# A gated linear attention layer: the first gates' Silu put behind the first tile of the second queries, and other shares of the heads' steps for queries and keys

## The chip, the cores and the metric

The kernel runs on one core of a Trainium2 chip. The core has engines that work side by side, each through a queue of its own in order: TensorE (PE; the profile lists the loading of its weights apart, as PEld), VectorE (DVE), ScalarE (ACT), GpSimd (POOL) and SyncE (SP), which here only issues transfers. The metric is the device time of one execution in microseconds (us), in which all times below are given.

## What is computed

The reference is a decoder trunk of two layers on 512 tokens of width 1024, in float32: a latent attention layer, a gated linear attention layer (GLA), each followed by a squared-ReLU MLP, and a last norm. The change lies in the GLA layer:

```
h = xn @ w_in                      # q 512, k 512, v 1024, g 1024, a 16 columns
gk = log_sigmoid(a @ w_gk_up + b_gk) / 16
# 4 heads of 128 (keys) x 256 (values); b = cumulated gk; state S carried over the tokens
o = (q * exp(b)) @ S + causal(sum_d q k exp(b_t - b_s)) @ v
o = rms_norm(o, g_norm) * silu(g)
x = x + o @ w_o
```

## The kernel before, in words

Each product of two float32 matrices is made of three matmuls of high and low parts (`mm3`, L129 to L134): ACT writes the high part (L124), DVE the low one (L127).

In `gla` the input is projected in six pieces, in the order "vgqkVG" (`proj`, L1773). "v" is the first half of the values; "g" the first half of the gates, as seven products of 256 columns (`seven`, L1336, matmuls of L1344) in place of eight; "q" and "k" are the second half of the queries and keys (`proj_qk(1)` and `proj_qk(3)`, two tiles of 24 matmuls of 512 columns each, L132 to L134, and a DVE copy out, L1463 or L1466); "V" the second half of the values, again by `seven`; "G" the second half of the gates. The first half of the queries and keys is projected ahead of all this.

"g" leaves its sums raw: `g_done` copies them to eight tiles of 128x256 (L1428). `silu` (L1434) later turns all eight, in place, by an activation each (L1436). Silu lies in another table of ACT than Exp and Ln; a table load stands ahead of the first of them, and `exp_set` (L138) loads the old table behind the last. Each of these instructions goes through `keep_in_program_order`, which pins it behind the instruction that was written just before it on its engine. Exp and Ln are held behind the latest `exp_set` (`act_e`, L141). For the other instructions the written order is a rank, not an order: an instruction that is ready may be placed ahead of one that is written earlier.

The heads' work (`heads`, L1791) is a second generator. It is cut into steps, and after each unit that `proj` yields the pace is raised by `PACE` (L38) of its piece and one step is taken for each whole unit of pace. Heads 0 and 1 come first, interleaved:

- steps 1 to 12: six stages of the attention inside 128 tokens, for head 0 and head 1 in turn: pairs, fours (2), fours (8), halves (32), halves (64), turned. A stage makes its operands, and its products are written with the step after it. In the halves ACT copies an operand (tile E, L1643; one buffer), PE multiplies it (L1651), and ACT copies the blocks into A (L1657). "Turned" transposes the keys (L149, L1677) and splits them into tiles kth and ktl.
- step 13: the last products. Steps 14 to 17: `states` 0 (nine matmuls with the turned keys, L132 to L134, and sums of L1716 and L1720 whose parts go to tile S), `own_tiles` 0 (L1727, into two banks of tag "b"), `states` 1, `own_tiles` 1 (a bank of tag "b" and one of tag "c").
- step 18: `silu`, then `past` 0 (nine matmuls of L1727 with S). Step 19: `gated` 0, where ACT squares the outputs from their banks (L1748) and DVE multiplies them by the gates (L1750). Step 20: `gates` 2 (the decays of head 2, one matmul of L1544 and then Abs, Exp and Ln) and `past` 1. Step 21: `gated` 1. Step 22: `gates` 3 and the norm of head 0. Step 23: that of head 1. Then heads 2 and 3 follow in the same way.

Tag "b" has three banks of PSUM. `own_tiles` of heads 0 and 1 take all three, and the "V" piece takes three for its sums (z, w, y; L1362). In `seven` the first product goes to z, and ACT copies z to y behind it (L1347).

With `PACE` at 3.75 for "q" and "k" the steps fall so: 1 to 6 in "v" and "g", 7 to 9 after the first query tile, 10 to 13 after the second, 14 to 17 after the first key tile, 18 to 21 after the second, 22 to 26 in "V", the rest in "G".

Of the kernel before, what the change touches and what calls it, by code (L numbers as in the profile page):

```python
# [34 lines left out]
HV = 256  # L35
RANK = 16
EPS = 1e-6
PACE = {"v": 0.4, "g": 0.6, "q": 3.75, "k": 3.75, "V": 0.75, "G": 2.1}  # L38

Q_PART = 0.75  # L40
SCALE = (Q_PART / (NOPE + ROPE)) ** 0.5
# [9 lines left out]
def trunk_kernel(ctx: ExitStack, tc: tile.TileContext, t_in: dict, out: bass.AP):  # L51
# [86 lines left out]
    def exp_set():  # L138
        table[0] = tc.keep_in_program_order(ACT.preload_act_table_set("natural_log_exp_and_others"))
# [1103 lines left out]
    def gla(layer, nrm, vtag, ytag):  # L1243
# [49 lines left out]
        def b_type(c0, hf, done):  # L1293
            banks = [bank("b"), bank("b"), bank("b"), bank("ac"[hf])]

            def mms(w, kk, k, t):
                xk = cut(X[k], slice(None), slice(t * P, (t + 1) * P))
                mm3(banks[t], xk, cut(w, slice(None), kk), k == 0, k == ND - 1)

            for kc in range(2):  # L1300
                raw = load(
                    w_in[kc * 512 : (kc + 1) * 512, c0 + hf * 512 : c0 + hf * 512 + 512].rearrange("(k p) n -> p k n", p=P), 4, 512
                )
                for g in range(2):
                    w = piece(raw[:, 2 * g : 2 * g + 2], 2, 512, at=AT_SEVEN)
                    k0 = kc * 4 + g * 2
                    if k0 + 2 < ND:
                        for kk in range(2):
                            for t in range(NT):
                                mms(w, kk, k0 + kk, t)  # L1310
                            yield
                    else:
                        for t in range(NT):
                            for kk in range(2):
                                mms(w, kk, k0 + kk, t)
                            done(t, banks[t])
                            if t % 2:
                                yield
# [84 lines left out]
        G = {}  # L1403

        def g_done(hf):
            def room():
                t = gp.tile([P, 2 * NT * HV], F32, tag="g", bufs=1, name=f"g{hf}")
                G[hf] = [t[:, i * HV : (i + 1) * HV] for i in range(2 * NT)]
                return t

            def done_tile(t, p):
                if t == 0:
                    G["room"] = room()
                with tc.high_priority():
                    tc.keep_in_program_order(
                        ACT.activation(G["room"][:, t * S : (t + 1) * S], p, AF.Silu, scale=rtok[:, t : t + 1])
                    )
                    if t == NT - 1:
                        exp_set()
                if t == NT - 1:  # L1420
                    gdone.add(hf)

            def done(c, th, p):
                if hf not in G:
                    room()
                for i in range(2):
                    src, dst = p[:, i * HV : (i + 1) * HV], G[hf][2 * (2 * th + i) + c]
                    ACT.activation(dst, src, AF.Copy, scale=-1.0 if c else 1.0)  # L1428
                if (c, th) == (1, 0):
                    gdone.add(hf)  # L1430

            return done_tile if hf else done

        def silu():  # L1434
            for n, s in enumerate(G[0]):
                tc.keep_in_program_order(ACT.activation(s, s, AF.Silu, scale=rtok[:, n // 2 : n // 2 + 1]))  # L1436
            exp_set()

        def residual_back():
            x = residual_room("xT_back")  # L1440
            xT[:] = [x[:, j] for j in range(ND)]
            xall_of[0] = x
            for j in range(ND):
                POOL.dma_start(x[:, j], kept[:, j])
# [65 lines left out]
        V = {}  # L1510

        def v_done(hf):
            def done_tile(t, p):
                hi, lo = slot(vtag), slot(vtag)
                r = rtok[:, t : t + 1]
                ACT.activation(hi, p, AF.Copy, scale=r)
                DVE.scalar_tensor_tensor(lo, p, r, f(hi), ALU.mult, ALU.subtract)
                for c in range(2):
                    V[2 * hf + c, t] = cut((hi, lo), slice(None), slice(c * HV, (c + 1) * HV))
                if t == NT - 1:  # L1520
                    vdone.add(hf)

            if hf == 0:
                return done_tile

            def done(c, th, p):
                hi, lo = slot(vtag), slot(vtag)
                r_all = rtok_n if c else rtok
                for i in range(2):
                    cs = slice(i * HV, (i + 1) * HV)  # L1530
                    r = r_all[:, 2 * th + i : 2 * th + i + 1]
                    ACT.activation(hi[:, cs], p[:, cs], AF.Copy, scale=r)
                    DVE.scalar_tensor_tensor(lo[:, cs], p[:, cs], r, f(hi[:, cs]), ALU.mult, ALU.subtract)
                    V[2 * hf + c, 2 * th + i] = cut((hi, lo), slice(None), cs)
                if (c, th) == (1, 0):
                    vdone.add(hf)

            return done
# [234 lines left out]
        def proj():  # L1773
            parts = {
                "v": lambda: b_type(2 * DK, 0, v_done(0)),
                "g": lambda: seven(2 * DK + D, 0, g_done(0), both, ahead=2 * DK + FB),
                "q": lambda: proj_qk(1),
                "k": lambda: proj_qk(3),
                "V": lambda: seven(2 * DK + FB, 1, v_done(1), both),
                "G": lambda: b_type(2 * DK + D, 1, g_done(1)),  # L1780
            }
            for c in "vgqkVG":
                for _ in parts[c]():
                    if c == "v":
                        next(forming, None)
                    yield PACE[c]
                if c == "V":
                    residual_back()


        def heads():  # L1791
            for h in (0, 2):
                while any(i not in qk for i in (h, h + 1, 4 + h, 5 + h)):
                    yield
                late = None
                for two in zip(levels(h), levels(h + 1)):
                    for stage in two:
                        products = stage()
                        if late:
                            late()  # L1800
                        late = products
                        yield
                        if h and turning and 1 in vdone:
                            gather(turning.pop(0))
                            yield
                late()
                yield
                while h // 2 not in vdone:
                    yield

                def run(*stages):
                    for stage, r in stages:
                        stage(r)
                        yield

                if h == 0:
                    while 0 not in gdone:
                        yield
                    yield from run((states, 0), (own_tiles, 0), (states, 1), (own_tiles, 1))
                    silu()  # L1820
                    yield from run((past, 0), (gated, 0))
                    gates(2)
                    yield from run((past, 1), (gated, 1))
                    gates(3)
                else:
                    yield from run((states, 2), (own_tiles, 2), (past, 2), (states, 3))
                    while 1 not in gdone:
                        yield
                    yield from run((gated, 2), (own_tiles, 3), (past, 3), (gated, 3))
                yield from run((head_norm, h), (head_norm, h + 1))  # L1830
                if h:
                    begun.append(out_start(w_o, Y, 3, "bca"))
                    yield from run((gather, h))
                    begun[0][2](4)
                    yield from run((gather, h + 1))

        begun, turning = [], [0, 1]
        forming = quadrants()
        both = [sb.tile([P, S], F32, tag="acc", bufs=2, name=uname("weight_sum")).rearrange("p (k n) -> p k n", n=TH) for _ in range(2)]
        fetch(2 * DK + D, both, *SUM_2)  # L1840
# [3 lines left out]
        for _ in rest:  # L1844
            pass
        gates(1)
        main, side = proj(), heads()
        pace = 0.0
        for units in main:
# [43 lines left out]
    O, begun = mla(0, nrm, w0, mla_pools)  # L1893
# [23 lines left out]
    psum_layout(False)  # L1917
    slot_layout(SLOT_AT, 8)
    Y, begun = gla(0, n_mix1, "V", "B")
    n_mlp1 = Norm(ND, inv_dr, "mlp", ND)  # L1920
    out_proj(t_in["gla_w_o"][0], Y, n_mlp1, begun)
# [59 lines left out]
```

## Time and profile before

| | us |
|---|---|
| median of 3 runs | 1043.01 (1042.83 to 1043.1) |
| the profiled execution | 1042.12 |
| its span, first to last instruction | 1040.4 |
| PE busy | 1026.6 |
| DVE busy | 898.5 |
| ACT busy | 713.0 |
| PE busy between 571 and 690, the GLA layer from the second queries on | 114.5 of 119 |

"Busy" is the time in which an engine has an instruction at work, as a sum over the span. Idle time of an engine that nobody waits for costs nothing; what counts is where PE stands still, and for whom. In the lines below, "out<-in" names the tiles that are written and read without their buffer numbers, L is the line of the kernel, "xN" a number of like instructions that the line takes together, and a bracket at the end gives the idle time before it and what ended it. Times in such lines are from the span's start.

### The profile page before, as it was taken

The numbers are of one execution on the slowest core, as the hardware profiler recorded it, in microseconds if no ns is written. First come the engines' busy times: TensorE is split into PE (matmuls) and PEld (weight loads), VectorE is DVE, ScalarE is ACT, GpSimd is POOL, SyncE is SP. The second block draws the span as 40 slices with busy tenths as digits, with TensorE's granted clock in tenths as the row PEclk, the third lists the DMA queues.
The fourth block names the chain that finished last, engine by engine and source line by source line (L and its number), as shares of the span: only waits on it lengthen the run. The fifth ranks groups of instructions, "written<-read, shape, count | busy, mean of one in ns | idle before, by whom it ended". The sixth has DMA issues, their size and how long they took to land.

```text
span 1040.4 us, 17339 instructions
## 1 busy us (share of the span) xinstructions
PE 1026.6 (99%) x6666; PEld 925.6 (89%) x6666; DVE 898.5 (86%) x1387; ACT 713.0 (69%) x1178; POOL 120.3 (12%) x160
## 2 busy tenths in 40 slices
PE   9999999999999999999999989999999999999997
PEld 7788888899999999998889888888989989989986
DVE  7889976999989989989698679579799999898994
ACT  8667754676776776785475594765677677677784
POOL 7400000400101001002112110000000000000000
PEclk9999999999999999999999999999999999999999
DMA  7401214778677777626648643344568777777422
GB/s 234 123 21 41 79 45 152 196 198 214 175 203 201 182 201 197 150 82 184 170 89 186 141 122 133 106 97 148 143 201 198 191 195 199 195 190 187 119 82 81
DMA packets 74082, 157.40 MB, mean 151 GB/s; under 512 B 10160, under 2 KB 43952, under 8 KB 71440
## 3 DMA queue, kind: packets, MB, share of 16 engines
q1 hardware_dynamic: 57184, 115.66, 34.6%
q0 software_dynamic: 14720, 38.80, 20.9%
q10 hardware_dynamic: 2096, 1.84, 0.6%
q8 instruction: 52, 0.85, 0.3%
q14 instruction: 30, 0.25, 0.1%
HBM read 151.83 MB, written 4.19 MB: 150 GB/s over the span
## 4 chain that ended last, share of the span: by engine, by line
PE 83%; DVE 7%; ACT 4%; DMA 4%; issue 1%; SPq 0%; ACTq 0%; DVEq 0%; POOLq 0%
PE ps L992 25%; PE ps L1012 13%; PE ps L1005 13%; PE ps L132 7%; PE ps L133 7%; PE ps L134 7%; PE ps L1180 2%; DMA wraw<-in_gla_w_in_dram 2%; DVE wl L127 2%; PE ps L149 1%; PE ps L1344 1%; PE ps L1214 1%; ACT wh L124 1%; PE ps L1601 1%; PE ps L1727 1%
## 5 line engine op out<-in xcount | busy, mean ns | idle before, releaser
L124 ACT ACTIVATE wh<-wraw 128x1024 fp32r<-128x1024 f32 x141 | 148.2, 1056 | 99.5 <-issue 38.6
L127 DVE TENSOR_TENSOR wl<-wraw,wh 128x1024 fp32r<-128x1024 f32 x141 | 172.0, 1221 | 25.2 <-ACT wh L124 24.2
L992 PE MATMUL ps<-T,wh 128*128 128x256 f32 x896 | 154.8, 275 | 0.3
L127 DVE TENSOR_TENSOR wl<-comb,wh 128x1024 fp32r<-128x1024 f32 x112 | 136.6, 1221 | 14.4 <-ACT wh L124 14.4
L124 ACT ACTIVATE wh<-comb 128x1024 fp32r<-128x1024 f32 x112 | 118.6, 1059 | 43.3 <-issue 30.0
L992 PEld LDWEIGHTS ps<-T,wh 128*128 128x128 f32 x896 | 135.0, 188 | 0.8 <-ACT ps L1022 0.3
L992 PE MATMUL ps<-T,wl 128*128 128x256 f32 x448 | 123.3, 275 | 0.0
L1012 PE MATMUL ps<-wh,set 128*128 128x512 f32 x392 | 122.1, 390 | 0.0
L992 PE MATMUL ps<-set,wh 128*128 128x256 f32 x672 | 116.9, 276 | 0.0
L132 PE MATMUL ps<-set,wh 128*128 128x512 f32 x280 | 110.0, 393 | 0.0
L133 PE MATMUL ps<-set,wh 128*128 128x512 f32 x280 | 109.7, 392 | 0.0
L134 PE MATMUL ps<-set,wl 128*128 128x512 f32 x280 | 109.6, 392 | 0.0
L1005 PE MATMUL ps<-hidden_parts,wh 128*128 128x256 f32 x784 | 105.8, 275 | 0.0
L992 PEld LDWEIGHTS ps<-set,wh 128*128 128x128 f32 x672 | 102.0, 188 | 0.5
L1005 PEld LDWEIGHTS ps<-hidden_parts,wh 128*128 128x128 f32 x784 | 96.6, 188 | 0.0
L992 PE MATMUL ps<-set,wl 128*128 128x256 f32 x336 | 92.5, 275 | 0.0
L1012 PEld LDWEIGHTS ps<-wh,set 128*128 128x128 f32 x392 | 73.6, 188 | 15.3
L992 PEld LDWEIGHTS ps<-T,wl 128*128 128x128 f32 x448 | 84.1, 188 | 0.0
L1012 PE MATMUL ps<-wl,set 128*128 128x512 f32 x196 | 76.3, 389 | 0.0
L992 PEld LDWEIGHTS ps<-set,wl 128*128 128x128 f32 x336 | 63.1, 188 | 0.0
L133 PEld LDWEIGHTS ps<-set,wh 128*128 128x128 f32 x280 | 52.6, 188 | 11.2 <-DVE set L1770 0.4
L134 PEld LDWEIGHTS ps<-set,wl 128*128 128x128 f32 x280 | 52.6, 188 | 11.1 <-DVE wl L127 0.2
(456 smaller groups left out, 2276.9 us busy)
## 6 DMA issues: line engine op xcount, KB each, us to landing
comb<-in_mlp_w_down_dram SPq DMA_DIRECT2D x74, 512.0 KB, 4.4
wraw<-in_mlp_w_up_dram SPq DMA_DIRECT2D x18, 1024.0 KB, 4.9
wraw<-in_mlp_w_up_dram SPq DMA_DIRECT2D x28, 512.0 KB, 5.6
comb<-in_mlp_w_down_dram POOLq DMA_DIRECT2D x28, 512.0 KB, 7.2
wraw<-in_gla_w_in_dram SPq DMA_DIRECT2D x8, 1024.0 KB, 5.3
comb<-in_mlp_w_up_dram SPq DMA_DIRECT2D x14, 512.0 KB, 4.6
comb<-in_mlp_w_up_dram POOLq DMA_DIRECT2D x14, 512.0 KB, 6.8
wraw<-in_mlp_w_up_dram POOLq DMA_DIRECT2D x14, 512.0 KB, 7.5
```

The source lines that it names most:

```text
L124: order(ACT.activation(hi, src, AF.Copy))
L127: lo_eng.tensor_tensor(lo, src, f(hi), ALU.subtract)
L132: PE.matmul(psum, wh, xh, start=start, stop=False)
L133: PE.matmul(psum, wh, xl, start=False, stop=False)
L134: PE.matmul(psum, wl, xh, start=False, stop=stop)
L149: PE.transpose(psum, src, ident[: src.shape[0], : src.shape[0]])
L992: PE.matmul(o, a_, x_, start=start and j == 0 and k == 0 and n == 0, stop=k == KH - 1 and n == 2, skip_group_check=True)
L1005: PE.matmul(o, w_[:, k, j * P : (j + 1) * P], x_[:, ts], start=opens, stop=k == 1 and n == 2, skip_group_check=True)
L1012: PE.matmul(o, x_, w_, start=start and k == 0 and n == 0, stop=k == 1 and n == 2, skip_group_check=True)
L1180: PE.matmul(p, a, x, start=k == 0 and n == 0, stop=k == 3 and n == 2)
L1214: PE.matmul(o, a, b_, start=False, stop=k == 3 and n == 2, skip_group_check=True)
L1344: PE.matmul(p, x_, w_[:, k], start=start and t == 0 and k == 0 and n == 0, stop=k == KH - 1 and n == 2, skip_group_check=True)
```

## The change

`silu` is no longer called in the heads' step 18. `proj` calls it once, after the first unit of "q": behind the first tile of the second queries and ahead of the steps that follow that tile. `PACE` becomes 4.25 for "q" and 3.25 for "k". The sum over both pieces stays 15. Steps 7 to 10 now fall after the first query tile, 11 to 14 after the second, 15 to 17 after the first key tile, 18 to 21 after the second, and all others where they fell.

```diff
-PACE = {"v": 0.4, "g": 0.6, "q": 3.75, "k": 3.75, "V": 0.75, "G": 2.1}
+PACE = {"v": 0.4, "g": 0.6, "q": 4.25, "k": 3.25, "V": 0.75, "G": 2.1}
...
                 for _ in parts[c]():
                     if c == "v":
                         next(forming, None)
+                    if c == "q" and not silent:
+                        silent.append(c)
+                        silu()
                     yield PACE[c]
...
                     yield from run((states, 0), (own_tiles, 0), (states, 1), (own_tiles, 1))
-                    silu()
                     yield from run((past, 0), (gated, 0))
...
-        begun, turning = [], [0, 1]
+        begun, turning, silent = [], [0, 1], []
```

## The prediction

> **What bounds the kernel now.** The head of the page comes first, then the busy time by stretch, then who TensorE (PE) waited for, then the order on each engine around those waits.
>
> ```profile
> span 1040.4 us, 17339 instructions
> PE 1026.6 (99%) x6666; PEld 925.6 (89%) x6666; DVE 898.5 (86%) x1387; ACT 713.0 (69%) x1178; POOL 120.3 (12%) x160
> ```
>
> PE works in 99% of the span. A change that takes no matmul away can win only where PE stands still. The stretches of the gated layer show where that is (instructions in brackets, then the granted clock, which is 1.00 in all of them).
>
> ```profile
> core 0: us, PE busy (x) PEld busy (x) DVE busy (x) ACT busy (x) POOL busy (x), PEclk, DMA share, GB/s
> 577.00:586.00 9.00, 8.88 (x48) 6.78 (x47) 6.86 (x10) 8.23 (x21) 2.21 (x2) 1.00 1.05 234
> ...
> 600.00:607.00 7.00, 4.97 (x27) 4.02 (x26) 2.13 (x5) 6.96 (x15) 0.00 (x0) 1.00 0.03 5
> 607.00:613.00 6.00, 4.97 (x42) 4.77 (x43) 5.35 (x14) 6.00 (x19) 0.00 (x0) 1.00 0.00 0
> 613.00:632.00 19.00, 19.00 (x157) 18.88 (x156) 18.93 (x53) 16.04 (x31) 4.31 (x8) 1.00 0.68 222
> 632.00:650.00 18.00, 17.60 (x88) 14.57 (x88) 17.21 (x43) 7.79 (x13) 0.00 (x0) 1.00 0.36 118
> ```
>
> PE stands 2.03 in 600 to 607 and 1.03 in 607 to 613, while ScalarE (ACT) is busy throughout. The waits of PE from 540 to 700 name both:
>
> ```profile
> engine line waited for: us in total, times, longest us
> PE ps L1344 <- DVE g L1750: 2.0, 1, 2.0
> PE ps L1344 <- ACT ps L1347: 1.0, 1, 1.0
> ```
>
> L1344 is the first product of the second value half ("V"), L1750 the gating of heads 0 and 1. The order on the engines says why (start, length, engine, line, what; idle time before it in brackets; PEld is the loading of weights):
>
> ```profile
> 599.53 0.41 ACT L124 ACTIVATE S<-tmp 128x256 fp32r<-128x256 f32 x1
> 599.95 1.28 ACT L1436 ACT_TABLE_LOAD   x1
> 601.25 3.31 ACT L1436 ACTIVATE g<-g,rtok 128x256 f32<-128x256 f32 x8
> 604.57 1.28 ACT L139 ACT_TABLE_LOAD   x1
> 605.87 0.38 ACT L1748 ACTIVATE tmp<-ps 128x256 f32<-128x256 f32 x1
> ...
> 610.25 0.60 ACT L1347 ACTIVATE ps<-ps 128x512 f32<-128x512 f32 x1
> ```
>
> ```profile
> 606.37 0.79 DVE L1750 TENSOR_TENSOR g<-ps,g 128x256 f32<-128x256 f32 x2 [2.35 <-ACT tmp L1748]
> ```
>
> ```profile
> 604.44 0.39 PE L1544 MATMUL ps<-tmp,tmp 96*128 96x512 f32 x1
> 606.86 0.38 PE L1344 MATMUL ps<-wh,set 128*128 128x256 f32 x1 [2.03 <-DVE g L1750]
> ...
> 610.91 0.39 PE L1344 MATMUL ps<-wh,T 128*128 128x256 f32 x1 [1.03 <-ACT ps L1347]
> ```
>
> ```profile
> 606.85 0.19 PEld L1344 LDWEIGHTS ps<-wh,set 128*128 128x128 f32 x1 [2.34 <-DVE g L1750]
> 610.90 0.19 PEld L1344 LDWEIGHTS ps<-wh,T 128*128 128x128 f32 x1 [1.23 <-ACT ps L1347]
> ```
>
> The eight Silu and their two table loads hold ACT for 1.28 + 3.31 + 1.28 = 5.87, from 599.95 to 605.85. Behind them stand the squares of L1748, which with L1750 empty the banks of the heads' outputs; V's first product needs one of those banks. PE has nothing else left at 604.83 and waits until 606.86. The block starts the moment the S split of 599.53 ends: that is the instruction written before it, behind which it is pinned.
>
> **Silu to the front (-2.03 and about -0.8).** The eight activations and two loads stay, 5.87 of ACT in all; they carry no DMA, so no queue of SP or POOL is passed. In the new place they are pinned behind the last ACT instruction written before them, the split of the second query tile's weights (563.69 below), and need the gates' copies (L1428), the last of which end at 571.06:
>
> ```profile
> 563.69 1.05 ACT L124 ACTIVATE wh<-wraw 128x1024 fp32r<-128x1024 f32 x1
> ...
> 570.43 0.63 ACT L1428 ACTIVATE g<-ps 128x256 f32<-128x256 f32 x2
> 570.96 1.05 ACT L124 ACTIVATE wh<-wraw 128x1024 fp32r<-128x1024 f32 x1
> 576.75 1.06 ACT L124 ACTIVATE wh<-wraw 128x1024 fp32r<-128x1024 f32 x1 [4.74 <-PE ps L133]
> 577.71 0.61 ACT L1643 ACTIVATE E<-qk 128x512 f32<-128x512 f32 x1
> ```
>
> From 572.01 to 576.75 ACT is idle (4.74). What PE next needs of ACT is the E copy of 577.71. The two weight splits of 570.96 and 576.75 can slide behind: they serve the second key tile and V. A whole block from 571.06 ends at 576.93, 0.78 ahead of the E copy, so its cover is ACT's own idle time. If that cover were gone, it would cost up to its 5.87 (rival B).
>
> At the old place everything from 605.87 on moves up by up to 605.87 - 599.95 = 5.92. The gating pair of L1750 would end near 601.2 instead of 607.16, and the bank is free about 3.6 before PE comes to ask for it. The first stall goes whole: 2.03 (2.34 by the weight loads, an upper end).
>
> For the second stall the bounds are 0 (ACT is again late with the copy of L1347, for which PE waits) and 1.03 (1.23 on the weight-load side). The first product ends at 610.91 - 1.03 = 609.88 and the copy begins at 610.25, when ACT comes free. The nearest row for what remains is the same place in the first gates, where the product behind the first one did not wait for the copy's end (549.46 + 0.58 = 550.04) but began at 549.75, read in the chain of waits and in ACT's order:
>
> ```profile
> 549.75 2.75 PE ps L1344 x24
> ```
>
> ```profile
> 549.46 0.58 ACT L1347 ACTIVATE ps<-ps 128x512 f32<-128x512 f32 x1
> ```
>
> I take 0.8, near the upper end, since ACT's queue at 607 is the Silu's backlog. What is late next is nothing on PE: in 613 to 632 it is busy in all 19.00. VectorE (DVE) is as full there (18.93), but had 4.87 idle in 600 to 607, so the gating and the second gates, which wait for the same block, move up with PE and its later work follows.
>
> On what a switch of tables costs, the row is 1.28 for the load, and the next activation starts at 601.25, 0.02 after it. The Trainium skill ("ScalarE: Activation LUTs", What ACT_TABLE_LOAD costs) adds a drain of about 1.38 us to each load. By it the block would be an estimated 8.63 instead of 5.87 and would not fit ahead of the E copy; this trace shows no such drain after either load.
>
> **The shares (about 0).** Adding the units up (front part), 4.25 and 3.25 move two steps by one place each: step 10 (last half-level of head 1: one DVE product, one E copy, and what head 0 has left from step 9: four matmuls, two copies, the split of A) ahead of the second query tile, and step 14 (the nine state products of head 0 with their sums and splits) ahead of the first key tile. Nothing is added and neither has a DMA. Rows on both sides of them:
>
> ```profile
> 578.09 0.39 PE L133 MATMUL ps<-set,wh 128*128 128x512 f32 x1
> 578.38 0.38 PE L1651 MATMUL ps<-E 128*128 128x128 f32 x1
> ```
>
> ```profile
> 585.27 0.48 PE L132 MATMUL ps<-set,wh 128*128 128x512 f32 x1
> ...
> 586.66 0.38 PE L132 MATMUL ps<-set,kth 128*128 128x256 f32 x1 [0.44 <-ACT kth L124]
> ```
>
> ```profile
> 587.27 1.01 DVE L127 TENSOR_TENSOR ktl<-ps,kth 128x384 fp32r<-128x384 f32 x2
> ```
>
> The order on PE is already that of readiness: E products stand inside the second query tile, and the first state product, written behind the first key tile, runs amid it. A place in the writing only breaks ties. For step 10 the bounds are about -0.3 and +0.3 (578.38 - 578.09 = 0.29 is such a gap); for step 14 they are -0.44 (its wait goes) and +2.1 (rival A). I take 0 for both, as the nearest rows show them interleaved.
>
> **Sum.** The profiled execution took 1042.12 (span 1040.4, 1.72 around it): 1042.12 - 2.03 - 0.8 = 1039.29. The median of the runs, 1043.01, lies 0.89 above that execution, so I forecast 1040.2. A measurement of this kernel can tell about 0.2% (2.1) from no change: faster is below 1040.9, slower above 1045.1.
>
> **The rivals.** *A, the states come too early:* all nine state products of step 14 stand ahead of the first key tile, and PE, which takes its queue in order, waits for the split of the turned keys. Head 0's half of it ends near 587.27 + 0.5 = 587.8; PE would stand from 585.27, 2.5 instead of 0.44. Gain 2.83 - 2.1 = 0.7: 1042.3, no change. For it: the share was moved, and that 0.44 wait exists. Against: the key products are ready and fill such gaps now.
>
> *B, slower: the block lands on the E copies.* From 577 to 586 ACT is busy in 8.23 of 9.00, because the halves' copies go back and forth with PE (L1643, L1651). If the block starts later than 577.71 - 5.87 = 571.84, every us delays the E copy, and PE stands at the L1651 which lies five matmuls into the second query tile. From a start at 574.7 the loss exceeds 2.83; whole, behind the split of 576.75, it is 5.87: 1042.12 - 2.83 + 5.87 + 0.89 = 1046.1. Against it: inputs are there at 571.06 and ACT idles then.
>
> *C, another wait takes the place:* V starts early, but the heads behind it do not keep up, because DVE is nearly full from 613 to 650 (18.93 and 17.21). If half of the 2.83 is given back in the second gates, 1041.6, no change. Against: DVE's idle time ahead of that.
>
> *D, the switch is longer than its rows:* were ACT to stand for another load's time, 1.28, at each of the two, the block of 8.43 would end at 579.49, 1.78 behind the E copy's start; gain 1.05, 1042.0. The start at 601.25 speaks against it. The skill's drain is of this kind and length.
>
> *E, no effect:* the block runs where it ran. 1043.0. The start right behind 599.53 says its written place decides, so hardly.
>
> **How the numbers follow.** Forecast 0.64, A 0.16, C 0.11, B 0.05, D 0.01, E 0.03. The forecast's own range is 1039.0 to 1040.9, from 2.1 to 4.0 (both stalls on the weight-load side, 3.57, and the 0.44). Another 0.5 for small gaps such as 0.29 gives the low end, 1038.5; the high end takes in A and C, 1042.4. Only B and tails stay outside. Faster 0.65 (the forecast and a little of C), same 0.29, slower 0.06.
>
> **What would show it.** Right: the Silu and both loads ahead of 577, no PE wait on L1750, V's first product directly behind the second gates' matmul near 604.8, the second wait under 0.4, and PE's order unchanged from 577 to 604. Wrong: PE waits on E (L1651) above 1 in 577 to 586 (B), a wait of 2 at the state products (A), or V's start early but its end not (C).

## The result and the profile after

The changed kernel takes 1039.48 (median of 22 runs, 1038.34 to 1045.51) against 1042.98 for the kernel before (22 runs, 1041.02 to 1045.69): a ratio of 0.9972, 95% interval 0.9964 to 0.9981, so 0.2 to 0.4% faster. Its profiled execution took 1039.04 with a span of 1037.3; the span of before was 1040.4, so the two profiles differ by 3.1. Three of the kernels below (silu_only, shares_only, block_x3) have one execution each of 1466 to 5905, which their ratios leave out and their medians hold; without it these medians are 1039.42, 1042.80 and 1041.32.

The head of the page after:

```profile
span 1037.3 us, 17338 instructions
PE 1025.9 (99%) x6666; PEld 926.3 (89%) x6666; DVE 898.5 (87%) x1387; ACT 713.6 (69%) x1178; POOL 121.2 (12%) x160
```

The work is the same (6666 matmuls, ACT 713.6 against 713.0). What went is time in which PE stood. The busy time by stretch, after:

```profile
core 0: us, PE busy (x) PEld busy (x) DVE busy (x) ACT busy (x) POOL busy (x), PEclk, DMA share, GB/s
600.00:607.00 7.00, 7.00 (x48) 6.37 (x46) 5.55 (x15) 5.65 (x17) 0.00 (x0) 1.00 0.21 31
607.00:613.00 6.00, 5.39 (x48) 5.19 (x47) 5.88 (x19) 6.00 (x16) 0.00 (x0) 1.00 0.23 50
613.00:632.00 19.00, 18.25 (x139) 17.34 (x137) 17.00 (x42) 14.71 (x27) 4.31 (x8) 1.00 0.62 208
632.00:650.00 18.00, 17.19 (x90) 14.81 (x91) 17.07 (x42) 4.84 (x8) 0.00 (x0) 1.00 0.35 116
```

From 600 to 607 PE is now busy throughout (4.97 before), and ACT, which was full, has 1.35 to spare. New is that PE loses 0.75 in 613 to 632 and 0.81 behind it, where it lost nothing and 0.40. The waits of PE from 540 to 700, after, name the three places that are left:

```profile
engine line waited for: us in total, times, longest us
PE ps L132 <- DVE set L1533: 1.6, 1, 1.6
PE ps L1344 <- DVE g L1750: 0.6, 1, 0.6
PE ps L132 <- ACT kth L124: 0.2, 1, 0.2
```

ACT's order after, first around the Silu's new place, then at the copy that PE used to wait for:

```profile
565.39 1.28 ACT L1436 ACT_TABLE_LOAD   x1
566.68 0.51 ACT L1436 ACTIVATE g<-g,rtok 128x256 f32<-128x256 f32 x1
568.30 1.06 ACT L124 ACTIVATE wh<-wraw 128x1024 fp32r<-128x1024 f32 x1 [1.11 <-DMA wraw<-in_gla_w_in_dram]
569.27 0.71 ACT L1428 ACTIVATE g<-tmp 128x256 f32<-128x256 f32 x2
569.88 0.61 ACT L1643 ACTIVATE E<-qk 128x512 f32<-128x512 f32 x1
570.40 0.63 ACT L1428 ACTIVATE g<-ps 128x256 f32<-128x256 f32 x2
570.93 2.90 ACT L1436 ACTIVATE g<-g,rtok 128x256 f32<-128x256 f32 x7
573.84 1.28 ACT L139 ACT_TABLE_LOAD   x1
575.13 1.07 ACT L124 ACTIVATE wh<-wraw 128x1024 fp32r<-128x1024 f32 x1
576.71 1.06 ACT L124 ACTIVATE wh<-wraw 128x1024 fp32r<-128x1024 f32 x1 [0.52 <-PE ps L133]
577.67 0.62 ACT L1643 ACTIVATE E<-qk 128x512 f32<-128x512 f32 x1
...
607.59 0.60 ACT L1347 ACTIVATE ps<-ps 128x512 f32<-128x512 f32 x1
```

The block is over at 575.12; the idle 4.74 ahead of 576.75 has shrunk to 0.52, and the E copy starts at 577.67, as before (577.71). PE at the places that count, after:

```profile
585.25 0.48 PE L1727 MATMUL ps<-set,ADh 128*128 128x256 f32 x2
...
604.09 0.39 PE L1544 MATMUL ps<-tmp,tmp 96*128 96x512 f32 x1
604.32 0.28 PE L1344 MATMUL ps<-wh,set 128*128 128x256 f32 x1
...
607.85 0.38 PE L1344 MATMUL ps<-wh,T 128*128 128x256 f32 x1 [0.61 <-DVE g L1750]
...
632.81 0.50 PE L132 MATMUL ps<-wh,set 128*128 128x512 f32 x1 [1.56 <-DVE set L1533]
```

Set beside the same matmuls of before, this is the account of the time. L1544 of the second gates: 604.44 to 604.09, -0.35. V's first product: 606.86 to 604.32, -2.54. Its second product: 610.91 to 607.85, -3.06. The last line's matmul belongs to the second half of the gates; before it stood at

```profile
634.92 0.50 PE L132 MATMUL ps<-wh,set 128*128 128x512 f32 x1 [0.25 <-DVE set L1533]
```

so the lead is down to 2.11 there: 0.95 was given back. When the same matmuls of both traces are paired, the lead is -2.65 from 664 on and -3.1 behind 980.

Why the 0.95 went is in ACT's order after, ahead of the wait at 632.81:

```profile
626.79 1.06 ACT L124 ACTIVATE wh<-wraw 128x1024 fp32r<-128x1024 f32 x1 [2.87 <-DMA wraw<-in_gla_w_in_dram]
627.75 0.89 ACT L1532 ACTIVATE set<-tmp,rtok 128x256 fp32r<-128x256 f32 x2
```

ACT stands 2.87 at a weight split of the second gates until its transfer has landed, and the copies of V (L1532, whose low parts DVE forms in L1533) stand behind it. The chain of waits has the transfer, of before

```profile
625.42 5.11 DMA wraw<-in_gla_w_in_dram
```

and of after:

```profile
618.97 7.71 DMA wraw<-in_gla_w_in_dram
```

It is issued 6.45 earlier and lands only 3.85 earlier, and the split that needs it now stands ahead of V's copies of 627.75. Before, the pair of copies of 628.80 stood ahead of that split, as ACT's order before shows:

```profile
628.80 0.91 ACT L1532 ACTIVATE set<-tmp,rtok 128x256 fp32r<-128x256 f32 x2 [1.84 <-DVE tmp L1352]
630.63 1.06 ACT L124 ACTIVATE wh<-wraw 128x1024 fp32r<-128x1024 f32 x1 [0.92 <-DMA wraw<-in_gla_w_in_dram]
```

### The profile page after: what moved, and what is told of

Same layout as the page of the kernel before. It is cut to its first block, busy times and chain, and to the rows that moved or that the text cites. A ratio compares the mean times of both kernels' runs of the same rounds, so it can differ in the third digit from the quotient of the medians.

```text
span 1037.3 us, 17338 instructions
## 1 busy us (share of the span) xinstructions
PE 1025.9 (99%) x6666; PEld 926.3 (89%) x6666; DVE 898.5 (87%) x1387; ACT 713.6 (69%) x1178; POOL 121.2 (12%) x160
## 4 chain that ended last, share of the span: by engine, by line
PE 88%; DVE 5%; ACT 4%; DMA 1%; issue 1%; ACTq 0%; SPq 0%; DVEq 0%
PE ps L992 25%; PE ps L1012 13%; PE ps L1005 13%; PE ps L132 8%; PE ps L133 8%; PE ps L134 8%; PE ps L1180 2%; PE ps L1344 2%; PE ps L149 1%; PE ps L1214 1%; DVE wl L127 1%; PE ps L1601 1%; PE ps L440 1%; ACT wh L124 1%; PE ps L1727 1%
```

## The experiments

The theory: moving the Silu alone gives the gain, as the squares of L1748 no longer stand behind them; the shares give about nothing; the part given back comes from ACT standing at a transfer with V's copies behind it. The rivals: the shares carry part of the gain; the block costs something in its new place; the part given back comes from DVE being full.

**The Silu alone: silu_only.**

```diff
-PACE = {"v": 0.4, "g": 0.6, "q": 4.25, "k": 3.25, "V": 0.75, "G": 2.1}
+PACE = {"v": 0.4, "g": 0.6, "q": 3.75, "k": 3.75, "V": 0.75, "G": 2.1}
```

> The new place of the Silu alone, the shares left at 3.75 and 3.75. Theory (the gain is the block that leaves the place ahead of the gating): V's first product starts right behind the second gates' matmul, the wait on L1750 ahead of it is gone, and 2.2 to 2.6 of the 3.5 are there; the place of the own-tile products stays as before, so the 0.35 that PE gained between 584 and 594 is missing: about 1039.8, 0.25 to 0.35% faster than before. Rival (the block and the shares only help together): under 1 us, and a wait on L1651 or on the state products takes the rest.

Measured: 1039.49 (before, beside it, 1042.39), ratio 0.9984 [0.997, 0.9999]; the profiled execution 1039.56. The wait of 2.03 for L1750 is 0.6, and the wait for L1533 is 1.6, as in the changed kernel. The interval is wide (four runs lie at 1041.38 to 1045.78), but the medians of this and of the changed kernel are equal, and so is what the profiles show at the stall: paired with before, the matmuls gain 2.29 across it here and 2.28 in the changed kernel.

**The shares alone: shares_only.** The kernel before with 4.25 and 3.25.

> The new shares alone, the Silu left in step 18. Theory: the own-tile products of head 0 stand ahead of the first key tile, PE gains some 0.3 there, the Silu still holds ScalarE and V waits about 2 for its bank: 1042.6, within 0.1% of before. Rival (the shares carry a part of the gain): over 1 us faster.

Measured: 1043.13 (before 1042.39), ratio 1.0006 [0.9996, 1.0015]. Waits of PE from 540 to 700:

```profile
PE ps L1344 <- DVE g L1750: 2.0, 1, 2.0
PE ps L132 <- ACT kth L124: 1.6, 1, 1.6
PE ps L1344 <- ACT ps L1347: 0.7, 1, 0.7
```

Both stalls are there: the shares remove neither. The wait for the turned keys has grown to 1.6, and ACT's order says by what:

```profile
586.42 1.06 ACT L124 ACTIVATE wh<-wraw 128x1024 fp32r<-128x1024 f32 x1 [1.54 <-DMA wraw<-in_gla_w_in_dram]
587.50 0.87 ACT L124 ACTIVATE kth<-ps 128x384 fp32r<-128x384 f32 x2
```

The turned keys stand behind V's second weight split, and this stands 1.54 for its transfer. In the kernel before the same split stood 0.47. Here, too, a split whose transfer is late holds up what is ready. The profiled execution took 1045.05 and is one of the two longest of the ten that the ratio compares, so it does not tell whether the shares had a part in the wait.

**No Silu at all: no_silu.** The changed kernel without the call: the eight activations and both loads are left out, so the first gates enter the outputs raw.

> The changed kernel with the eight Silu and both table loads left out, so the first gates enter the product raw and unscaled. It shows what the block still costs at its new place. Theory (it lies in idle time of ScalarE): within 0.5 us of the changed kernel, about 1039.2, the same wait of 1.6 at the start of the second gates. Rival (a part of the block delays the E copies or the splits behind it): 1 to 3 us faster than the changed kernel.

Measured: 1039.02 (before 1042.39), ratio 0.9968 [0.9956, 0.998]; the profiled execution 1039.62. Paired with before, V's first product is 2.63 early (by the paired median) and the stretch behind its second 3.04; in the changed kernel these are 2.63 and 3.05. In the new place 5.9 of ACT cost PE nothing up to there. The wait for L1533 is 0.8 here, where the same 1.6 was expected; why is not shown, and the profiled execution is not shorter for it.

**The second gates' splits behind V's copies: pin_g.** The changed kernel, and

```diff
-                    w = piece(raw[:, 2 * g : 2 * g + 2], 2, 512, at=AT_SEVEN)
+                    with tc.issue_after(last_v[0].ins) if hf and kc else nullcontext():
+                        w = piece(raw[:, 2 * g : 2 * g + 2], 2, 512, at=AT_SEVEN)
...
-                    ACT.activation(hi[:, cs], p[:, cs], AF.Copy, scale=r)
+                    last_v[:] = [ACT.activation(hi[:, cs], p[:, cs], AF.Copy, scale=r)]
```

> The changed kernel, with the splits of the second half of the second gates' weights (the ones that wait for a transfer until 626.8) issued behind the last copy of V's results on ScalarE. Theory (the 1.0 that is given back at 630 is ScalarE's queue standing at a split whose weights have not landed, with V's copies behind it): the wait of 1.6 on L1533 falls under 0.5 and the kernel gains 0.6 to 1.2 over the changed one, about 1038.4. Rival (the bank is late because VectorE is full there): the wait stays over 1 and the time does not move.

Measured: 1038.44 (before 1042.39), ratio 0.9969 [0.9956, 0.9982]; the profiled execution 1037.83, span 1035.7. All its waits of PE from 540 to 700 (lines stand one lower than in the changed kernel):

```profile
PE ps L1345 <- DVE g L1751: 0.6, 1, 0.6
PE ps L132 <- ACT kth L124: 0.2, 1, 0.2
```

The wait for L1533 is gone, although DVE is busier from 613 to 632 than in the changed kernel (18.55 of 19.00 against 17.00). So it came from ACT's order, not from DVE being full. The span is 1.6 shorter than that of the changed kernel's profile, but the intervals of the two ratios overlap, so a gain in the median is not shown.

**A longer block: block_x3.** Before each Silu, two more into a spare tile: 16 more activations, about 6.6 of ACT.

```diff
+            spare = tmp((P, HV))
             for n, s in enumerate(G[0]):
+                for _ in range(2):
+                    tc.keep_in_program_order(ACT.activation(spare, s, AF.Silu, scale=rtok[:, n // 2 : n // 2 + 1]))
```

> The changed kernel with two more Silu of the same tile into a spare tile ahead of each of the eight: 16 more activations, 6.6 more of ScalarE in the block, still pinned in a row. It takes the block's cover away. Theory (the block is free only as long as it ends ahead of the E copy of 577.7): its later part lies between the E copies, TensorE waits there (L1651) or at what follows the halves, 2 to 5 in all, and the kernel is 2 to 5 slower than the changed one, 1041.5 to 1044.5. Rival (the products of queries and keys cover any such delay): under 1 slower.

Measured: 1041.38 (before 1042.71), ratio 0.999 [0.998, 0.9999]; the changed kernel on the same chip took 1038.89. Waits of PE (lines stand three lower):

```profile
PE ps L1654 <- ACT E L1646: 1.6, 3, 0.7
PE ps L132 <- DVE set L1536: 1.5, 1, 1.5
PE ps L1344 <- DVE g L1753: 0.4, 1, 0.4
```

Once the block outgrows the idle time ahead of the E copies, PE waits for E: three times, 1.6 in all. It costs 2.5, not its whole length: the Silu and the E copies are interleaved on ACT. In the profiles, paired with the changed kernel of after_again, 2.3 of it are lost between 577 and 600.

**The block one tile later: silu_second.** The call comes behind the second tile of the queries.

```diff
-                    if c == "q" and not silent:
+                    if c == "q":
                         silent.append(c)
-                        silu()
+                        if len(silent) == 2:
+                            silu()
```

> The changed kernel with the block behind the second query tile instead of the first, where it stands on ScalarE between the last copies of the halves and the split of the turned keys (near 585). The turned keys come some 5 later; 12 own-tile products and most of the first key tile stand ahead of the state products on TensorE, about 6 of work. Theory (what counts is that the block is out of the way of the gating, and that products cover it): within 1 of the changed kernel, about 1039.7. Rival (only ScalarE's idle stretch ahead of 577 can take it): 3 or more slower than the changed kernel, with a wait on kth or ktl of that size.

Measured: 1038.78 (before 1042.71), ratio 0.9959 [0.9946, 0.9973]; waits 1.5 for L1533, 0.4 for kth, 0.2 for L1750. Either place will do; what counts is that the block is off ACT when the gating comes.

**Both splits pinned: pin_both.** pin_g, and V's second weight split behind the turned keys:

```diff
-            product(w, cut_in(s1), "T1", True)
+            with tc.issue_after(last_k[-1].ins) if hf else nullcontext():
+                s1 = cut_in(s1)
+            product(w, s1, "T1", True)
...
-                    split(p, *at["k"])
+                    split(p, *at["k"], order=last_k.append)
```

> As pin_g, and the split of V's second weights (the one that waits for its transfer near 585) issued behind the splits of the turned keys on ScalarE. Theory (runs differ by 2 because that transfer lands early or late and the turned keys stand behind it): the wait on kth is gone in every run, the median falls by another 0.3 to 1, to 1037.4 to 1038.1, and the runs lie closer together. Rival (the spread has another cause): median and spread of pin_g, 1038.4, with runs at 1041.

Measured: 1038.0 (1037.6 to 1039.44; before 1042.71), ratio 0.9955 [0.9942, 0.9967]. One wait of PE is left from 540 to 700, 0.6 for the gating. It is the best version, 0.9 under the changed kernel beside it, though the intervals overlap.

**The changed kernel beside these: after_again.**

> The changed kernel as it is, beside the others on the same chip: 1039.5, with some runs near 1041. If the profile falls on one of those, theory says that the wait on kth (L132) in it is about 2 and that the split ahead of kth waited for its transfer.

Measured: 1038.89 (before 1042.71), ratio 0.9969 [0.9956, 0.9981], with single runs of 1040.82 and 1041.66. The profiled execution is one of 1038.83 and waits 0.2 for kth, so the expectation for a longer one was not put to the test.

**A late transfer: late_load and late_load_pinned.** The first transfer of V's second weights is issued twice, once in the changed kernel and once in pin_both:

```diff
             fetch(base, a11, (0, 0))
+            if hf:
+                fetch(base, s1, SUM_1[0])
             fetch(base, s1, *SUM_1)
```

> The changed kernel, in which the first transfer of V's second weights is issued twice, so that the sum for which ScalarE's split waits near 585 lands one transfer (5 to 8) later. Nothing computed changes. Theory (the turned keys stand behind that split on ScalarE, and the states behind them on TensorE): a wait on kth of 4 to 7 and 1043 to 1046, 4 to 6 slower than the changed kernel. Rival (TensorE has other work there): under 1 slower.

Measured: 1043.18 (before 1042.13), ratio 1.001 [1.0001, 1.0019]. ACT and then PE, in late_load:

```profile
587.29 1.06 ACT L124 ACTIVATE wh<-wraw 128x1024 fp32r<-128x1024 f32 x1 [2.69 <-DMA wraw<-in_gla_w_in_dram]
588.38 0.88 ACT L124 ACTIVATE kth<-ps 128x384 fp32r<-128x384 f32 x2
```

```profile
588.92 0.38 PE L132 MATMUL ps<-set,kth 128*128 128x256 f32 x1 [2.78 <-ACT kth L124]
```

ACT stood 2.69 for the transfer, and PE waited 2.78 behind it for the split of keys that were ready. The wait is shorter than the 4 to 7 that were expected, and yet the kernel loses some 4 against the changed kernel; the rest is shown in the last section.

> The same late transfer in the kernel of pin_both, where the split stands behind those of the turned keys. Theory: no wait on kth, 1038.0 to 1038.6, within 0.6 of pin_both, since V needs these weights only near 607. Rival (the transfer itself is late for V, or crowds the others): 2 or more slower than pin_both.

Measured: 1038.01 (before 1042.13), ratio 0.9961 [0.9948, 0.9974]. ACT, in late_load_pinned:

```profile
586.27 0.87 ACT L124 ACTIVATE kth<-ps 128x384 fp32r<-128x384 f32 x2 [0.67 <-PE ps L149]
588.55 1.06 ACT L124 ACTIVATE wh<-wraw 128x1024 fp32r<-128x1024 f32 x1 [1.41 <-DMA wraw<-in_gla_w_in_dram]
```

The same late transfer costs nothing when the split that needs it stands behind the keys.

**The old shares in the best version: pin_both_old_shares.** 3.75 and 3.75 in pin_both.

> pin_both with the shares of before, 3.75 and 3.75. With the turned keys out of the transfer's way, theory gives the shares 0.3 or nothing: 1038.0 to 1038.5. Rival (the shares are worth more once the split is out of the way): 1039 or more.

Measured: 1038.02 (before 1042.13), ratio 0.996 [0.9948, 0.9973], against 1038.0 and 0.9955 with the new shares: no difference that can be measured.

**The changed kernel once more: after_third.** Of 28 executions of the changed kernel, 7 have a mean granted clock of 0.997 and take 1040.8 to 1041.7; the median of the other 21 is 1039.04, though four of these, too, take 1040.66 to 1045.51. This run was for the place of those 2 us.

> The changed kernel once more, for the place of the 2 us by which some of its runs are longer: 13 of its 22 first runs lie at 1038.3 to 1039.9 with a mean granted clock of 0.998 or 0.999, 9 at 1040.7 to 1045.5, six of these with 0.997. If the long runs come from the turned keys' split standing behind V's second weight split and its transfer, a long run (1040.7 to 1041.7) shows PE waiting for kth by 1.5 to 2.8 near 586, and with a wait near 2.8 also the clock at 0.5 for some 3.4 us behind it, as the run with the late load did; a short run shows 0.2 to 0.5 there and no such fall. The rival: the long runs stand elsewhere, for one at the start of the second gate half (a wait for L1533 above 1.6 near 631), and kth stays at 0.2 to 0.5 in a long run too.

Measured: 1039.31, clock 0.999, with 0.2 for kth and 1.5 for L1533: a short run again, so it tells nothing of the long ones. All 20 executions of the four kernels in which the turned keys do not stand behind a transfer (silu_second, pin_both, late_load_pinned, pin_both_old_shares) lie below 1039.9. That, and late_load, make the wait for kth the likely place. The wait for L1533 alone is not it: pin_g, which has it no more, still has runs of 1041.41, 1041.47 and 1044.92, and silu_second, which has it (1.5), has none above 1039.8. No profile of a long execution of the changed kernel was taken, so it stays open.

## Why the prediction was right, and where it was not

The forecast was 1040.2, measured 1039.48; the sum for the profiled execution was 1039.29, measured 1039.04. Of the two gaps, 0.25 lies in the sum. The rest is the distance between profiled execution and median, 0.89 in the kernel before and 0.44 in this one.

- **First stall, -2.03.** Right in mechanism and place: V's first product starts at 604.32, directly behind L1544. Without the -0.35 that L1544 itself gained, it is 2.54 - 0.35 = 2.19, between the 2.03 of the matmuls and the 2.34 of the weight loads. The experiment with the Silu alone shows the cause.
- **Second stall, -0.8.** Over-sized: V's second product gained 3.06 - 2.54 = 0.52, and 0.61 of waiting is left, where "under 0.4" was said. The step that failed is the comparison with the first gates. There no outputs of heads hold the banks that the piece needs; here the product now waits for another gating, the one that ended just ahead of 607.85. DVE, after:

```profile
607.37 0.42 DVE L1750 TENSOR_TENSOR g<-ps,g 128x256 f32<-128x256 f32 x1
```

  The copy of L1347, which it waited for before, starts at 607.59 and is not over when the product starts. Why the product needed the end of that copy before and does not need it now, the traces do not show.
- **The block in its new place, 0.** Right: no_silu gains nothing over it. But the start was wrong: the first Silu runs at 566.68, as its gates are ready then, not all eight from 571.06. The order is a pin behind one instruction, not a call to run together, so a weight split (568.30), gate copies and an E copy (569.88) could slip in.
- **The shares, 0.** Right in the time, wrong in the order: "PE's order unchanged from 577 to 604" failed. At 585.25, where the first key tile began (585.27), PE now runs head 0's own tiles (L1727), and the wait for the turned keys is 0.18 instead of 0.44. That is within -0.35 in this profile and in no measured time. Nor need the shares have brought it: in silu_only, with the old shares and the old order, no wait for the turned keys is listed at all, and the same matmuls gain 0.44 between 577 and 595.
- **Rival A, the states too early.** It did not come in the changed kernel (0.2 for kth). Its wait exists, in shares_only (1.6) and late_load (2.8), but by another way than was said: not as the keys are split too late for the order, but as their split stands behind one that waits for a transfer.
- **Rival B, the block on the E copies.** Not here. block_x3 shows that its mechanism is real and that its price, taken at the block's whole length, was too high: 6.6 more of ACT cost 2.5.
- **Rival C, another wait takes the place.** It came in part: "what is late next is nothing on PE" failed. The wait for L1533 gave back 0.95 of 3.06. Its cause was not the one named, DVE being full, but ACT at a transfer (pin_g). That the total was still right has to do with gains behind it that the prediction did not have: the lead grew again from 2.11 to 2.65 by 664, where a wait of 0.4 for E that PE had before is missing, and to 3.1 by the end, whose cause is open. The span's gain is thus 0.35 + 2.19 + 0.52 - 0.95 + 0.99 = 3.10, where 2.03 + 0.8 = 2.83 was said: three of the five terms were not in the forecast, and that they nearly cancel is luck.
- **Rival D, a longer switch.** No: both loads take 1.28, and the next activation starts within 0.02 (565.39 + 1.28 and 566.68; 573.84 + 1.28 and 575.13). The drain of about 1.38 that the Trainium skill ("ScalarE: Activation LUTs", What ACT_TABLE_LOAD costs) adds is not seen here; the loads of the kernel before (599.95, 604.57) are followed as closely.

## What to carry to other kernels

A block that nobody waits for (here table loads and activations whose results are needed some 25 us later) belongs where its engine idles, and what it is worth is read from the wait of the bounding engine at the old place, not from its length. After such a move look at each in-order queue for an instruction whose transfer has not landed: it holds up everything ready behind it, and putting it behind the ready work made a late transfer cost nothing here (1038.01 in late_load_pinned against 1043.18 in late_load). Where a second wait follows closely on the one removed, ask which other holders of the same banks are still ahead of it, before taking a price from a place where there are none.

## What the runs showed of the hardware that was not expected

A stand of PE can cost more than its length. The stretches around the wait of 2.78 in late_load:

```profile
core 0: us, PE busy (x) PEld busy (x) DVE busy (x) ACT busy (x) POOL busy (x), PEclk, DMA share, GB/s
586.00:589.00 3.00, 0.22 (x3) 0.08 (x1) 0.62 (x1) 1.68 (x3) 0.00 (x0) 1.00 1.22 188
589.00:592.40 3.40, 3.40 (x15) 3.21 (x16) 1.54 (x3) 0.25 (x1) 0.00 (x0) 0.53 0.11 16
592.40:596.00 3.60, 3.60 (x19) 3.06 (x18) 1.78 (x5) 1.99 (x5) 0.00 (x0) 0.97 0.00 0
```

Right behind it the granted clock is at about half for 3.4 and then full again; paired with the changed kernel of after_again, the loss grows from 2.5 at 586 to 4.0 at 588 and stays there. Behind the 2.03 of before and the wait of 1.62 for the turned keys in shares_only no such fall is in the profiles (the clock is 1.00 in both). But shares_only, which has the Silu where the kernel before has it, shows one behind its stand of 2.03 ahead of V's first product, the very stall that the change removes:

```profile
606.00:608.40 2.40, 0.37 (x3) 0.12 (x2) 0.60 (x2) 2.39 (x6) 0.00 (x0) 1.00 0.00 0
608.40:611.90 3.50, 3.50 (x17) 3.50 (x18) 2.91 (x6) 3.39 (x10) 0.00 (x0) 0.51 0.00 0
```

Paired with before, which has the same stand without the fall, its loss grows there from 1.4 to 3.0. The Trainium skill ("TensorE: Matmul & The Clock Gate", What's actually happening) gives an idle window of about 3.4 us, free-running, for a fall to half clock; the length at half clock agrees. Here 2.78 of standing was enough, and 2.03 was enough once and not another time. So a stall of this size can carry a surcharge of some 1.5 us, which a sum of PE's waits alone cannot hold, and the first stall may have been worth more than its 2.03 in some executions. How often the kernel before pays it stays open: of 61 executions of it that were run beside the experiments, 25 have a mean granted clock of 0.997 or less and a median of 1042.87, the other 36 one of 1041.87, but the profiled one is of the second kind (0.998).
